# Triangular inverses of the RWKV-7 part: 32-blocks by substitution, or 16-blocks by substitution joined on TensorE

## The chip, the cores and the metric

The kernel runs on one core of a Trainium2 chip. The metric is the device time of one execution in microseconds (us). The kernel before takes 1602.5 us (median of three runs, 1602.16 to 1603.44). Its profile is one execution taken by the hardware profiler.

## What is computed

One layer of a hybrid decoder: a projection of 1024 tokens feeds an RWKV-7 head group (8 heads of 64) and an S5 state-space group. Their outputs are projected and added to the residual, and a SwiGLU FFN follows. The change touches only the recurrence of the RWKV-7 heads:

```
def step(S, inp):
    r_t, w_t, k_t, v_t, a_t, b_t = inp
    sa = einsum("bhvk,bhk->bhv", S, a_t)
    S = S * w_t[:, :, None, :] + sa[..., None] * b_t[:, :, None, :] + v_t[..., None] * k_t[:, :, None, :]
    y = einsum("bhvk,bhk->bhv", S, r_t)
    return S, y
_, y = lax.scan(step, S0, xs)
```

The kernel takes this recurrence in chunks of 64 tokens. Within a chunk the terms `sa` depend on each other through a strictly lower triangular 64x64 matrix, and the kernel needs the inverse of the unit triangular matrix belonging to it: for each of 8 heads and 16 chunks, so 128 inverses of 64x64.

## The kernel before

The tokens are taken in four quarters of 256 (`qt` 0 to 3), each with 4 chunks. A quarter has 16 units of two heads each (`u`; `h2` is the head within it), so 32 matrices of 64x64. For a quarter, `prepare` forms queries, keys and values, `post` does the rest before the chain of chunks, and `chains` then walks the four chunks one after another with small matmuls (`chunk`). Within `post` the steps are:

- `amats` (L942) forms the triangular matrices on TensorE in the tile `ak`, and `l_write` (L973) writes them to `l_d` in DRAM.
- `token_major` (L959) transposes keys and values on TensorE.
- `solve` (L980) loads from `l_d` the diagonal 32-blocks into `LU`, one block to a row. A block has 32 columns of its inverse, and two rows take 16 columns each, so 64 blocks fill 128 rows. A forward substitution of 31 steps follows, with a product (L995) and a sum (L997) in each: 62 instructions, each waiting for the one before. Quarters 0 and 1 run it on VectorE (DVE), quarters 2 and 3 on GpSimd (POOL) (L991). The inverse `X` and its transposed copy `VT` (L998) go to `x_d` in DRAM (L999, L1000).
- `rest` (L1002) loads them back with another layout (four DMAs, L1009 and L1010): a block's rows lie in 32 partitions, so that TensorE can use them. It joins two 32-blocks to a 64-block with two sets of 32 matmuls (`pG` L1017, `pO` L1027), ScalarE (ACT) evacuating both, and writes the result over the matrix in `ak` (L1032, L1035).

All loads and stores named here are issued by one queue, that of SyncE (SP), in order. Each engine works its instructions in order too. That order is fixed when the program is built, by a planner that simulates the engines' times; the text of the program gives the priority. Around the four solves the program weaves other work: quarter 0 with the second half of the input projection (`pz` matmuls of `zhalf`, L268) and S5 units; quarter 1 with the chain of quarter 0, the S5 gate (`pglu`) and the conditioning sums (`acc`, L293 and L295, of weights `wada`); quarters 2 and 3 with the first half of the FFN (`pgate`, `pup`, `pdn`, all at L268; L1352 evacuates `pdn` on DVE, L1382 takes `pup`).

PSUM has eight banks. `rest` draws its bank by `ps_g` (L111): the one bank `g`, or `g` and `G` in turn in one part of the run.

## Time and profile before

| What | Value |
|---|---|
| time, median of three runs | 1602.5 us |
| span of the profiled execution | 1598.3 us |
| PE, DVE, ACT, POOL busy | 1416.4, 988.7, 551.9, 540.9 us |

The profiled execution's span is 4.2 us under the median of the runs, which also hold what lies around the span. How to read the rows below: a timeline row gives the start, the busy time and the instruction, `x64` meaning 64 of them merged; in brackets stands the idle time just before on that engine and what ended it. `PEld` is TensorE's weight load, `PE` its matmul. A float32 matmul stands as two records, so the 32 matmuls of `pG` are 64. In rows by stretch, the first number is the stretch's length, then each engine's busy time with its instructions in brackets, then the granted TensorE clock (1.00 is full), the busy share of the DMA engines and GB/s.

### The profile page before, as it was taken

What the parts mean: (1) busy time and instruction counts of PE and PEld (TensorE: products, weight loads), DVE (VectorE), ACT (ScalarE), POOL (GpSimd) and SP (SyncE); (2) the same over time, 40 slices, a digit from 0 to 9 for tenths busy, and PEclk for the clock granted to TensorE, in tenths of its full rate; (3) what the DMA queues carried; (4) which work ended last, traced back from release to release, by engine and by line L of the source; (5) the groups of instructions that cost most, each with busy time, mean ns of one, the idle gap of its engine ahead of it and who ended that gap; (6) DMA issues with size and microseconds to landing.
All of it is one profiled execution on the core that took longest, in us unless ns stands there. A gap on an engine that the chain in (4) does not pass through costs nothing.

```text
span 1598.3 us, 23239 instructions
## 1 busy us (share of the span) xinstructions
PE 1416.4 (89%) x9167; PEld 1146.8 (72%) x9167; DVE 988.7 (62%) x1687; ACT 551.9 (35%) x881; POOL 540.9 (34%) x452
## 2 busy tenths in 40 slices
PE   3897798897958878698999999899997999999997
PEld 3675576776747756576777777677786888888885
DVE  5959458889686889854448855345626433433335
ACT  4341234344245653233225422224443222222223
POOL 4358344443053333145000003400251254444543
PEclk9897999999878989799999999899999999999999
DMA  9424674353454356353223224422831433232331
GB/s 277 146 79 143 171 233 152 109 134 100 93 161 129 122 177 196 115 116 97 66 67 113 86 88 106 97 68 68 222 104 50 137 93 105 81 105 92 99 99 53
DMA packets 266220, 189.78 MB, mean 119 GB/s; under 512 B 71670, under 2 KB 237184, under 8 KB 266112
## 3 DMA queue, kind: packets, MB, share of 16 engines
q1 hardware_dynamic: 264624, 186.65, 39.7%
q8 instruction: 72, 1.18, 0.3%
q0 software_dynamic: 816, 0.57, 0.2%
q10 hardware_dynamic: 672, 1.08, 0.2%
q14 instruction: 36, 0.29, 0.1%
HBM read 159.20 MB, written 31.16 MB: 119 GB/s over the span
## 4 chain that ended last, share of the span: by engine, by line
PE 56%; DVE 22%; DMA 8%; issue 5%; POOL 5%; ACT 2%; SPq 2%; DVEq 0%; POOLq 0%; ACTq 0%
PE pup L268 14%; PE pgate L268 13%; PE pdn L268 13%; PE pz L268 3%; DMA wada<-in_w_ada_dram 3%; PE p L1051 3%; DVE acc L295 2%; POOL XU L997 2%; POOL stmp L995 2%; PE pu L365 2%; PE po L1303 2%; DVE zo L864 1%; DVE stmp L995 1%; PE pA L951 1%; DVE XU L997 1%
## 5 line engine op out<-in xcount | busy, mean ns | idle before, releaser
L268 PE MATMUL pdn<-wd,act 128*128 128x512 f32 x1056 | 269.1, 397 | 0.7 <-DVE x L1352 0.6
L268 PE MATMUL pup<-h,hl_up 128*128 128x512 f32 x1056 | 268.6, 397 | 0.2 <-ACT hl_up L131 0.2
L268 PE MATMUL pgate<-h,hl_g 128*128 128x512 f32 x1056 | 264.1, 396 | 1.2 <-ACT hl_g L131 1.2
L1352 DVE TENSOR_TENSOR x<-pdn,x 128x512 f32<-128x512 f32 x176 | 119.0, 688 | 185.8 <-PE pdn L268 185.2
L268 PEld LDWEIGHTS pup<-h,hl_up 128*128 128x128 f32 x1056 | 198.1, 189 | 45.9 <-issue 2.6
L268 PEld LDWEIGHTS pdn<-wd,act 128*128 128x128 f32 x1056 | 196.6, 189 | 47.4 <-DVE x L1352 2.1
L268 PEld LDWEIGHTS pgate<-h,hl_g 128*128 128x128 f32 x1056 | 196.6, 188 | 47.4 <-issue 3.6
L268 PE MATMUL pz<-hT,hl_z 128*128 128x256 f32 (+1 forms) x1008 | 184.7, 340 | 37.0 <-ACT zt L859 20.8
L268 PEld LDWEIGHTS pz<-hT,hl_z 128*128 128x128 f32 x1008 | 154.7, 202 | 63.6 <-ACT zt L859 25.5
L1387 DVE TENSOR_TENSOR rawd<-rawd,gfb 128x1024 f32<-128x1024 f32 x44 | 54.9, 1248 | 101.2 <-DMA rawd<-in_ffn_w_down_dram 80.5
L1303 PE MATMUL po<-wo,yhl 128*128 128x512 f32 x384 | 99.1, 412 | 3.7 <-ACT wo L131 1.5
L131 ACT CAST hl_up<-raw_up 128x1024 fp32r<-128x1024 f32 x44 | 46.2, 1051 | 129.3 <-PE pup L268 110.2
L1303 PEld LDWEIGHTS po<-wo,yhl 128*128 128x128 f32 x384 | 74.6, 198 | 22.4 <-ACT wo L131 2.2
L131 ACT CAST wd<-rawd 128x1024 fp32r<-128x1024 f32 x44 | 45.7, 1049 | 117.6 <-DVE rawd L1387 86.8
L863 POOL TENSOR_TENSOR zo<-zt 128x512 f32<-128x512 f32 x28 | 40.9, 1461 | 109.9 <-ACT zt L859 107.2
L295 DVE SCALAR_TENSOR_TENSOR acc<-wada,cact,acc 128x256 f32<-128x256 f32 (+1 forms) x112 | 71.3, 644 | 5.4 <-DMA wada<-in_w_ada_dram 4.1
L127 POOL TENSOR_TENSOR yhl<-yt,yhl 128x512 fp32r<-128x512 f32 x16 | 23.9, 1494 | 149.4 <-ACT yhl L1288 144.1
L127 POOL TENSOR_TENSOR hl_g<-raw_g,hl_g 128x1024 fp32r<-128x1024 f32 x19 | 45.7, 2407 | 81.3 <-ACT hl_g L131 73.0
L1381 ACT ACTIVATE sgt<-pgate 128x512 f32<-128x512 f32 x44 | 26.4, 599 | 133.9 <-PE pgate L268 133.8
L995 POOL TENSOR_TENSOR stmp<-LU,XU 128x126 f32<-128x126 f32 (+22 forms) x62 | 28.0, 451 | 129.3 <-DMA LU<-l_d 124.6
L127 POOL TENSOR_TENSOR wd<-rawd,wd 128x1024 fp32r<-128x1024 f32 x19 | 50.4, 2654 | 54.6 <-ACT wd L131 54.6
L127 POOL TENSOR_TENSOR hl_up<-raw_up,hl_up 128x1024 fp32r<-128x1024 f32 x19 | 50.8, 2676 | 51.7 <-ACT hl_up L131 51.7
(372 smaller groups left out, 2453.6 us busy)
## 6 DMA issues: line engine op xcount, KB each, us to landing
raw_g<-in_ffn_w_gate_dram SPq DMA_DIRECT2D x44, 512.0 KB, 3.7
raw_up<-in_ffn_w_up_dram SPq DMA_DIRECT2D x44, 512.0 KB, 3.8
rawd<-in_ffn_w_down_dram SPq DMA_DIRECT2D x44, 512.0 KB, 3.5
wada<-in_w_ada_dram SPq DMA_DIRECT2D x64, 256.0 KB, 3.2
raw_z<-in_w_in_dram SPq DMA_DIRECT2D x28, 512.0 KB, 4.2
wada<-in_w_ada_dram SPq DMA_DIRECT2D x16, 512.0 KB, 7.9
wraw<-in_w_out_dram SPq DMA_DIRECT2D x32, 256.0 KB, 4.1
zt_d<-zo SPq DMA_DIRECT2D x28, 256.0 KB, 2.3
```

The source lines that it names most:

```text
L127: (eng or G).tensor_tensor(out=out, in0=a, in1=b, op=ALU.subtract)
L131: S.copy(dst[:, 0], src)
L268: PE.matmul(ps, lhsT=lf(a, k), rhs=rf(b, k), start=(n == 0), stop=(n == 3 * kb - 1))
L295: V.scalar_tensor_tensor(out=acc, in0=wt, scalar=cact[:, k:k + 1], in1=acc, op0=ALU.mult, op1=ALU.add)
L365: PE.matmul(pu[hf, b], lhsT=uw[b][:, a_, k, :], rhs=hT[hf, k][:, b_, :], start=(k == 0 and n == 0), stop=(k == 7 and n == 2))
L863: G.tensor_tensor(out=o, in0=zt[:, 0:HT], in1=zt[:, 1:HT + 1], op=ALU.subtract)
L995: SOLVE.tensor_tensor(out=t, in0=LU[:, j, j + 1:32].unsqueeze(2).to_broadcast([P, nt, nk]), in1=X[:, j:j + 1, 0:nk].to_broadcast([P, nt, n ...
L997: SOLVE.tensor_tensor(out=X[:, j + 1:32, 0:nk], in0=X[:, j + 1:32, 0:nk], in1=t, op=ALU.add)
L1051: PE.matmul(ps[r, h], lhsT=a, rhs=b, start=(n == 0), stop=(n == len(ops) - 1))
L1303: PE.matmul(pss[i], lhsT=yh[k][:, a, 128 * i:128 * i + 128], rhs=wo[:, b], start=(k == 4 and n == 0), stop=(k == 3 and n == 2))
L1352: V.tensor_tensor(out=t, in0=ps, in1=t, op=ALU.add)
L1387: V.tensor_tensor(out=raw, in0=raw, in1=gfb, op=ALU.mult)
```

## The change

`solve` takes 16-blocks: 128 rows hold the 128 diagonal 16-blocks of a quarter, all 16 columns of a block in its row. The substitution has 15 steps (30 instructions) on 16x16 tiles and runs on DVE in all four quarters. `LU` comes by one DMA with pieces of 64 bytes; `X` and its transpose are written to `x_d` by four DMAs with pieces of 64 bytes, into the diagonal halves of 32-blocks. `x_d` is now one buffer for all quarters, filled with zeros at the start by two DMAs of the POOL queue. `rest` loads two tiles with two DMAs, then joins 16-blocks to 32-blocks: `blocks` issues 64 matmuls of 32x32, four positions along the diagonal of the PE array, into one PSUM bank. It is called three times (`pH`, `pX`, `pV`), and DVE takes each result out, the first with a mask `mlow` made at the start by four POOL selects. After that `pG` and `pO` follow as before. Comments are removed as well.

```
+    mlow = const.tile([P, 32], F32, name="mlow")
+    V.memset(mlow, 0.0)
+    for b in range(4):
+        G.affine_select(out=mlow[32 * b:32 * b + 32, 0:16], in_=mlow[32 * b:32 * b + 32, 0:16], ..., fill=1.0)
...
-    x_d = dram.tile([4, 2, 65536], F32, name="x_d")
+    x_d = dram.tile([2, P, HT], F32, name="x_d")
...
+    zero = pp.tile([P, HT], F32, name="zero")
+    G.memset(zero, 0.0)
+    for n in range(2):
+        nc.gpsimd.dma_start(x_d[n], zero)
     s5_params(*s5q)
...
     def solve(qt):
-        LU, tmp = t_("LU", [P, 32, 32]), t_("stmp", [P, 256])
-        for o in range(2):
-            nc.sync.dma_start(LU[64 * o:64 * o + 64], l_d[qt][:, 0:2048].rearrange("r (i t) -> r i t", t=64)[:, :, 0:32])
+        LU, tmp, X, VT = t_("LU", [P, 16, 16]), t_("stmp", [P, 64]), t_("X16", [P, 16, 16]), t_("V16", [P, 16, 16])
+        nc.sync.dma_start(LU, l_d[qt].rearrange("r (x n) -> (r x) n", x=2)[:, 0:1024]
+                          .rearrange("r (i t) -> r i t", t=64)[:, :, 0:16])
...
-        SOLVE = V if qt < 2 else G
-        for j in range(31):
-            nt, nk = 31 - j, j // 2 + 1
+        for j in range(15):
+            nt, nk = 15 - j, j + 1
             t = tmp[:, 0:nt * nk].rearrange("p (a b) -> p a b", b=nk)
-            SOLVE.tensor_tensor(out=t, in0=LU[:, j, j + 1:32]..., in1=X[:, j:j + 1, 0:nk]..., op=ALU.mult)
-            SOLVE.tensor_tensor(out=X[:, j + 1:32, 0:nk], in0=X[:, j + 1:32, 0:nk], in1=t, op=ALU.add)
-        SOLVE.tensor_copy(VT.rearrange("p k i -> p i k"), X)
-        nc.sync.dma_start(x_d[qt, 0].rearrange("(r n) -> r n", r=P), X.rearrange("p i k -> p (i k)"))
-        nc.sync.dma_start(x_d[qt, 1].rearrange("(r n) -> r n", r=P), VT.rearrange("p k i -> p (k i)"))
+            V.tensor_tensor(out=t, in0=LU[:, j, j + 1:16]..., in1=X[:, j:j + 1, 0:nk]..., op=ALU.mult)
+            V.tensor_tensor(out=X[:, j + 1:16, 0:nk], in0=X[:, j + 1:16, 0:nk], in1=t, op=ALU.add)
+        V.tensor_copy(VT.rearrange("p k i -> p i k"), X)
+        for n, w in enumerate((X, VT)):
+            d = x_d[n].rearrange("(r s) (i k) -> s r i k", s=2, k=32)
+            for s_ in range(2):
+                nc.sync.dma_start(d[s_, :, :, 16 * s_:16 * s_ + 16], w[s_::2])
...
     def rest(qt):
-        for o in range(2):
-            src = x_d[qt, :, 32768 * o:32768 * o + 32768]
-            nc.sync.dma_start(XB[:, :, 16 * o:16 * o + 16], src[0].rearrange("(u p k) -> p u k", u=16, k=16))
-            nc.sync.dma_start(VB[o::2], src[1].rearrange("(u p i) -> p u i", u=16, i=32))
+        for n, w in enumerate((XB, VB)):
+            nc.sync.dma_start(w, x_d[n].rearrange("(u b) (i k) -> (b i) u k", u=16, k=32))
...
+        def blocks(nm, lf, rf):
+            ps = ps_g(nm).rearrange("p (u k) -> p u k", k=32)
+            for u in range(16):
+                for b in range(4):
+                    r = slice(32 * b, 32 * b + 32)
+                    PE.matmul(ps[r, u, :], lhsT=lf(r, u, b), rhs=rf(r, u), start=True, stop=True,
+                              tile_position=(32 * b, 32 * b))
+            return ps
+        ps = blocks("pH", lambda r, u, b: aks[u // 8][r, u % 8, 0, 0, 32 * (b % 2):32 * (b % 2) + 32], lambda r, u: XB[r, u, :])
+        V.tensor_tensor(out=GT, in0=ps, in1=mlow.unsqueeze(1).to_broadcast([P, 16, 32]), op=ALU.mult)
+        ps = blocks("pX", lambda r, u, b: VB[r, u, :], lambda r, u: GT[r, u, :])
+        V.tensor_tensor(out=XB, in0=ps, in1=XB, op=ALU.add)
+        ps = blocks("pV", lambda r, u, b: GT[r, u, :], lambda r, u: VB[r, u, :])
+        V.tensor_tensor(out=VB, in0=ps, in1=VB, op=ALU.add)
```

## Rows read from the trace of the kernel before

**Rows 1.** The page's busy times of the whole span, with their shares and instruction counts.

```profile
PE 1416.4 (89%) x9167; PEld 1146.8 (72%) x9167; DVE 988.7 (62%) x1687; ACT 551.9 (35%) x881; POOL 540.9 (34%) x452
```

**Rows 2.** Busy time by stretch, all engines: the stretches with solves 0 and 1 and what follows, then those with solves 2 and 3.

```profile
340.00:400.00 60.00, 49.57 (x371) 41.99 (x371) 59.17 (x112) 26.66 (x47) 31.55 (x16) 0.91 0.40 110
400.00:432.00 32.00, 29.58 (x242) 25.84 (x242) 21.93 (x61) 4.53 (x11) 2.20 (x3) 0.90 0.32 70
432.00:500.00 68.00, 45.72 (x671) 39.19 (x671) 51.38 (x130) 30.04 (x70) 28.14 (x42) 0.72 0.57 147
500.00:660.00 160.00, 127.55 (x1112) 99.68 (x1112) 139.82 (x278) 75.54 (x141) 57.75 (x50) 0.88 0.53 165
740.00:760.00 20.00, 14.96 (x179) 11.30 (x179) 8.48 (x13) 5.59 (x7) 3.06 (x10) 0.83 0.68 159
760.00:1018.00 258.00, 258.00 (x1627) 203.45 (x1620) 157.03 (x235) 85.06 (x120) 30.67 (x60) 1.00 0.30 87
1018.00:1040.00 22.00, 14.28 (x182) 11.75 (x181) 6.62 (x12) 4.26 (x8) 1.92 (x5) 0.77 0.48 96
```

**Rows 3.** The chain that ended last: its shares by line in the stretch 335 to 395 us and in 395 to 500 us.

```profile
by line: DVE stmp L995 16.6%; DVE f L736 9.8%; DVE L L729 9.4%; issue 8.6%; DVE XU L997 7.4%; DVE tm L968 5.8%; DVE zo L864 4.3%; PE pz L268 3.6%; DVE tm L725 3.3%; DVE kn L252 2.4%; DVE L L728 2.2%; DVE th L895 2.0%; DVE L L726 2.0%; DVE k
...
by line: PE pz L268 13.1%; DVE XU L997 12.0%; DVE stmp L995 9.0%; PE pY L752 7.0%; DMA wada<-in_w_ada_dram 6.7%; PE pA L951 5.4%; SPq L769 4.1%; PE pY L749 3.5%; PE pglu L268 3.3%; DMA VT<-x_d 3.2%; DMA l_d<-ak 2.9%; DVE acc L293 2.8%; DVE 
```

**Rows 4.** Busy time by stretch of the products alone (L995) for the four solves, then of the sums alone (L997) for solves 0 and 1: DVE, POOL, then the clock, DMA share and GB/s.

```profile
340.00:441.00 101.00, 14.71 (x31) 0.00 (x0) 0.88 0.43 103
441.00:482.50 41.50, 11.55 (x31) 0.00 (x0) 0.70 0.49 153
708.00:742.00 34.00, 0.00 (x0) 14.39 (x31) 1.00 0.30 83
982.00:1019.20 37.20, 0.00 (x0) 13.59 (x31) 1.00 0.24 74
...
340.00:441.00 101.00, 9.36 (x31) 0.00 (x0) 0.88 0.43 103
441.00:482.50 41.50, 14.79 (x31) 0.00 (x0) 0.70 0.49 153
```

**Rows 5.** Timeline of single instructions of solve 0: the last six, back to back; then one beside a POOL instruction, and one of like size alone.

```profile
424.19 0.21 DVE L995 TENSOR_TENSOR stmp<-LU,XU 128x45 f32<-128x45 f32 x1
...
425.33 0.18 DVE L997 TENSOR_TENSOR XU<-XU,stmp 128x16 f32<-128x16 f32 x1
...
389.49 2.82 POOL L127 TENSOR_TENSOR hl_z<-raw_z,hl_z 128x1024 fp32r<-128x1024 f32 x1
390.00 2.46 DVE L995 TENSOR_TENSOR stmp<-LU,XU 128x136 f32<-128x136 f32 x1
...
397.78 0.29 DVE L997 TENSOR_TENSOR XU<-XU,stmp 128x136 f32<-128x136 f32 x1
```

**Rows 6.** Busy time by stretch of `pG` alone (L1017) in quarters 1 and 2: PE, PEld, then the granted clock, DMA share and GB/s. Then the timeline of `pG`'s matmuls in all four quarters, with the wait before each.

```profile
489.00:491.00 2.00, 1.20 (x64) 1.09 (x64) 1.00 0.52 66
749.00:752.00 3.00, 1.92 (x64) 1.81 (x64) 0.50 0.95 199
...
432.55 1.20 PE L1017 MATMUL pG<-XU,ak 32*32 32x32 f32 x64 [1.66 <-DMA XU<-x_d]
489.59 1.20 PE L1017 MATMUL pG<-XU,ak 32*32 32x32 f32 x64 [1.42 <-DMA XU<-x_d]
749.59 1.92 PE L1017 MATMUL pG<-XU,ak 32*32 32x32 f32 x64 [5.04 <-DMA XU<-x_d]
1025.98 1.92 PE L1017 MATMUL pG<-XU,ak 32*32 32x32 f32 x64 [7.72 <-DMA XU<-x_d]
```

**Rows 7.** Timeline of FFN weight loads just after those two long waits, and one group some us later; then one group that changes the tile shape between FFN matmuls.

```profile
751.43 5.76 PEld L268 LDWEIGHTS pup<-h,hl_up 128*128 128x128 f32 x19
1028.87 3.02 PEld L268 LDWEIGHTS pdn<-wd,act 128*128 128x128 f32 x9
1031.93 1.57 PEld L268 LDWEIGHTS pup<-h,hl_up 128*128 128x128 f32 x7
...
757.55 0.73 PEld L890 LDWEIGHTS pw<-wzk,wa 64*128 64x128 f32 x4 [0.35 <-issue]
```

**Rows 8.** A PSUM evacuation with a mask on DVE (minimum, median and maximum in ns of all 32), and the transposed copy of solve 0.

```profile
L953 DVE TENSOR_TENSOR ak<-pA,mask x32: 673/686/692, 281.6 to 971.4; 128x512 f32<-128x512 f32 x32
...
425.55 0.61 DVE L998 COPY VT<-XU 128x512 f32<-128x512 f32 x1
```

**Rows 9.** DMA issues (count, KB each, median us from issue to landing), then the SP queue's own time for one issue (ns, minimum, median, maximum) of `x_d`'s writes and of the loads into `LU`.

```profile
LU<-l_d SPq DMA_DIRECT2D x8, 256.0 KB, 4.7
XU<-x_d SPq DMA_DIRECT2D x8, 128.0 KB, 4.5
...
L999 SPq DMA_DIRECT2D x_d<-XU x4: 325/338/339, 425.5 to 1019.1; - x4
...
L987 SPq DMA_DIRECT2D LU<-l_d x8: 592/872/1767, 339.0 to 976.1; - x8
```

**Rows 10.** Timeline of POOL in the start-up: four mask selects, four DMA issues, and the idle time before a later instruction.

```profile
3.59 0.92 POOL L151 TENSOR_SCALAR_AFFINE_SELECT mask<-mask 64x64 f32<-64x64 f32 x4
...
122.24 2.15 POOL L638 DMA_DIRECT2D dcol<-in_s_d_dram  x4
...
96.35 2.40 POOL L127 TENSOR_TENSOR hl_z<-raw_z,hl_z 128x1024 fp32r<-128x1024 f32 x1 [7.26 <-ACT hl_z L131]
```

More of the change, by code (lines that the diff above doesn't have):

```diff
@@ L159 @@
         V.memset(rm[32 * b:32 * b + 32, b % 2:b % 2 + 1], 1.0)
+    mlow = const.tile([P, 32], F32, name="mlow")
+    V.memset(mlow, 0.0)
+    for b in range(4):
+        G.affine_select(
+            out=mlow[32 * b:32 * b + 32, 0:16], in_=mlow[32 * b:32 * b + 32, 0:16], pattern=[[0, 16]], base=16,
+            channel_multiplier=-1, compare_op=ALU.is_gt, fill=1.0,
+        )
     m01 = const.tile([P, HT], F32, name="m01")
@@ L982, in solve @@
         t_ = lambda nm, sh: RP[0].tile(sh, F32, tag=nm, name=nm)
-        LU, tmp = t_("LU", [P, 32, 32]), t_("stmp", [P, 256])
-        X, VT = (RP[0].tile([P, HT], F32, tag=nm, name=nm) for nm in ("XU", "VT"))
-        X, VT = X.rearrange("p (i k) -> p i k", k=16), VT.rearrange("p (k i) -> p k i", i=32)
-        for o in range(2):
-            nc.sync.dma_start(LU[64 * o:64 * o + 64], l_d[qt][:, 0:2048].rearrange("r (i t) -> r i t", t=64)[:, :, 0:32])
-        G.memset(X, 0.0)
-        for o in range(2):
-            G.memset(X[64 * o:64 * o + 64].rearrange("p i k -> p (i k)")[:, 16 * o:512:33], 1.0)
@@ L999, in solve @@
-        nc.sync.dma_start(x_d[qt, 0].rearrange("(r n) -> r n", r=P), X.rearrange("p i k -> p (i k)"))
-        nc.sync.dma_start(x_d[qt, 1].rearrange("(r n) -> r n", r=P), VT.rearrange("p k i -> p (k i)"))
-    def rest(qt):
-        XB, VB, GT = (t.rearrange("p (u k) -> p u k", k=32) for t in
-                      [RP[0].tile([P, HT], F32, tag=nm, name=nm) for nm in ("XU", "VT")] + [tr("GT")])
-        for o in range(2):
-            src = x_d[qt, :, 32768 * o:32768 * o + 32768]
-            nc.sync.dma_start(XB[:, :, 16 * o:16 * o + 16], src[0].rearrange("(u p k) -> p u k", u=16, k=16))
-            nc.sync.dma_start(VB[o::2], src[1].rearrange("(u p i) -> p u i", u=16, i=32))
-        aks = [sts[qt, q]["ak"] for q in range(2)]
+        LU, tmp, X, VT = t_("LU", [P, 16, 16]), t_("stmp", [P, 64]), t_("X16", [P, 16, 16]), t_("V16", [P, 16, 16])
@@ new lines, in solve @@
+        nc.sync.dma_start(LU, l_d[qt].rearrange("r (x n) -> (r x) n", x=2)[:, 0:1024]
+                          .rearrange("r (i t) -> r i t", t=64)[:, :, 0:16])
+        G.memset(X, 0.0)
+        G.memset(X.rearrange("p i k -> p (i k)")[:, 0:256:17], 1.0)
+        for j in range(15):
+            nt, nk = 15 - j, j + 1
+            t = tmp[:, 0:nt * nk].rearrange("p (a b) -> p a b", b=nk)
+            V.tensor_tensor(out=t, in0=LU[:, j, j + 1:16].unsqueeze(2).to_broadcast([P, nt, nk]),
+                            in1=X[:, j:j + 1, 0:nk].to_broadcast([P, nt, nk]), op=ALU.mult)
+            V.tensor_tensor(out=X[:, j + 1:16, 0:nk], in0=X[:, j + 1:16, 0:nk], in1=t, op=ALU.add)
@@ new lines, in solve @@
+        V.tensor_copy(VT.rearrange("p k i -> p i k"), X)
[3 more added lines that the diff above has]
+                nc.sync.dma_start(d[s_, :, :, 16 * s_:16 * s_ + 16], w[s_::2])
+    def rest(qt):
+        XB, VB = (t_.rearrange("p (u k) -> p u k", k=32) for t_ in
+                  [RP[0].tile([P, HT], F32, tag=nm, name=nm) for nm in ("XU", "VT")])
+        GT = tr("GT").rearrange("p (u k) -> p u k", k=32)
+        for n, w in enumerate((XB, VB)):
+            nc.sync.dma_start(w, x_d[n].rearrange("(u b) (i k) -> (b i) u k", u=16, k=32))
+        aks = [sts[qt, q]["ak"] for q in range(2)]
+        def blocks(nm, lf, rf):
[12 more added lines that the diff above has]
+        V.tensor_tensor(out=VB, in0=ps, in1=VB, op=ALU.add)
@@ L1020, in rest @@
             p0 = 64 * h2 + 32
-            S.copy(GT[p0:p0 + 32].rearrange("p u (k o) -> p u o k", o=2),
-                   ps[p0:p0 + 32].rearrange("p u (o k) -> p u o k", o=2))
+            S.copy(GT[p0:p0 + 32], ps[p0:p0 + 32])
         ps = ps_g("pO").rearrange("p (u k) -> p u k", k=32)
```

2 lines of the change are left out of this document (removed).

## The prediction

> **What bounds the kernel now.** I read the page's busy times first. PE is busy 1416.4 of 1598.3 us, DVE 988.7, POOL 540.9 [rows 1]. Those are means over stages with different limits, so next I cut the run into stretches around the solves [rows 2]. From 340 to 400 us DVE works 59.17 of 60 us and PE idles 10.4: DVE ends last. From 400 to 432 PE works 29.58 of 32: PE ends last. From 432 to 660 neither is full; DVE works 51.38 of 68 and 139.82 of 160, and latencies and loads lie between. From 740 to 1040 PE is busy throughout but for two holes: 5.04 us in 740 to 760 and 7.72 us in 1018 to 1040. The chain that ended last says the same with names [rows 3]: in 335 to 395 it is mostly DVE, and the solve's two lines hold 16.6% and 7.4% of it; in 395 to 500 it starts on `pz` and `pA` of PE, and later the solve of quarter 1 holds 12.0% and 9.0%. Solves 2 and 3 matter in another way: POOL works at them through 34 and 37 us [rows 4] while PE has FFN matmuls to do, and only the tail shows, as `pG` waiting for the loaded inverses [rows 6].
>
> So the change has two halves. In quarters 0 and 1 it takes work from an engine that is the bound. In quarters 2 and 3 it takes work from an idle engine (POOL) and gives some to PE, which is the bound.
>
> **Early: quarters 0 and 1.** Solve 0 costs DVE 14.71 + 9.36 = 24.07 us in 62 instructions, solve 1 11.55 + 14.79 = 26.34 [rows 4], and the transposed copy 0.61 us in solve 0 [rows 8]. Afterwards there are 30 instructions of at most 64 elements. The cheapest price is the step of the last small ones, six from 424.19 to 425.51: some 0.22 us each, so 6.6 us [rows 5]. The dearest is the present mean, 26.34 / 62 = 0.42 us: 12.7 us. The mean lies so far above the bottom because an instruction that meets a POOL instruction can take far longer: 2.46 us beside a POOL instruction of 2.82 us, where one of equal size takes 0.29 [rows 5]. POOL's other work stays, so I take a middle price of 0.33 us: 10 us per solve. Half the present copy comes to 0.3 us, and three PSUM evacuations of 0.69 us like that of `pA` to 2.1 [rows 8]. DVE pays 12.4 us instead of about 24.7 and 27: 12 and 15 us less.
>
> Not all of it is on the path. Of solve 0 the chain holds 24% of 60 us, 14.4 us, up to 395 [rows 3]. The 30 new instructions would mostly fall in that same stretch, at 10 us, so 4.4 us are won there. The rest of solve 0 lies beside PE's `pz` work and wins nothing. On the other side the joins of quarter 0 may land in that PE-bound stretch of 400 to 432; today `pG` runs after it. They cost at most 6.7 us (worked out below), and I take 2 us as exposed. Quarter 0 gives -2 us, with -10 (PE's whole idle time to 400) and +7 as ends.
>
> Of solve 1 the chain holds 21% of 105 us, 22 us. In its place come 10 us of solve, 0.3 of copy and 2.1 of evacuations: -9.6. Two delays stand against it. The DMAs: `X` and its copy now leave by four issues with 64-byte pieces instead of two; nothing in the trace writes such pieces, so I bound an issue by a write of long rows (0.34 us) below and a median issue into `LU` (0.87 us) above [rows 9]: 0.7 to 2.8 us more of SP's queue, behind which weight loads such as `wada` wait, which hold 6.7% of the chain from 395 to 500 [rows 3]. The two loads of 256 KB that replace four of 128 KB take the landing time of `LU` (4.7 us) against 4.5, and half the issues. I take +1.5. The joins: a set of matmuls, a hand-over, 0.69 us of DVE and a hand-over, three times, about 10 us more before `ak` is ready. But the solve now takes 41.5 us from first to last instruction [rows 4], and with 38% of its DVE time it should end 15 to 20 us sooner; that covers the 10. Quarter 1 gives -8 us, with -15 (all of DVE's saving) and 0 as ends. Early sum: -10.
>
> **Late: quarters 2 and 3.** PE's added work is three sets of 64 matmuls per quarter, 128 records each. Today's 64 records take 1.09 us of weight loads at full clock, 17 ns each, 1.81 at half [rows 6]. They alternate between two positions of the array; the new sets use four, which no row shows. If four overlap twice as well, a set takes 1.1 us; if not, 2.2; at half clock 3.6. I take 2.2, the nearest row: 6.7 us per quarter, 13.4 for both (6.6 to 21.6). Each set also cuts into a row of FFN matmuls, twice; a cut costs up to 0.35 us of unexplained issue time [rows 7]. Six sets and twelve cuts are 4.2 us at most; some sets will follow each other, so I take 2.
>
> The Trainium skill, "TensorEngine Tiling (Array Packing)", section Key Properties, says that a change of the tiling mode, not just of the tile, drains TensorE. That speaks against small sets amid 128x128 matmuls; the gap of 0.35 us before the 64-row group agrees in kind [rows 7]. If every change cost it, late would come out about 2 us dearer.
>
> Won back are the two waits of `pG` for the inverses, 5.04 and 7.72 us, and what follows them at half clock: 19 loads in 5.76 us and 9 in 3.02, against 0.224 us each in the group at 1031.93 [rows 7], 1.5 and 1.0 us, and 0.7 us for each `pG`: 3.9. Together 16.7 us. Why did PE wait? The planner put `pG` where it thought the data would be there, and POOL was late. The two quarters whose solves run on DVE waited only 1.66 and 1.42 us [rows 6]. With solves 2 and 3 on DVE, and POOL nearly empty from 760 to 1018 (30.67 us, solve 3 nearly alone [rows 2]), I expect waits of some 2.5 us each, new small ones at `pX`, `pV` and `pG` included, since each now waits for a DVE instruction in order behind FFN instructions. Won: 12 us. So late: +13.4 + 2 - 12 = +3.4.
>
> DVE itself takes on some 10 us per quarter there: it works 157.03 of 258 us from 760 to 1018 [rows 2], so the work is covered by idle time; uncovered it would cost 20. The new waits on DVE are the ones for `LU` and for the three sets: behind each stand `pdn`'s evacuations, and then PE, whose FFN has one bank each for `pgate` and `pup` and two for `pdn`. I add 0.6 us. Late sum: +4 (-10 to +16).
>
> The Trainium skill, "SBUF — State Buffer", section SBUF: two separate sides, says that VectorE instructions with two SBUF inputs and GpSimd instructions lock each other out of one port pair for a whole instruction. The 2.46 us agree [rows 5]. By that rule alone late solves on DVE cost the bottom price, 6.6 us.
>
> **Start-up.** Four more selects on POOL, 0.92 us for four like them, and two DMA issues on POOL's queue, 0.5 us each by the four issues of 2.15; POOL idles 7.26 us before 96.35 [rows 10]. Cover: DMA waits and that idle time. I put 0; uncovered, 0.9 + 1.1 + a memset, 2.5 us.
>
> **The sum.** -10 + 4 = -6 us: 1592.3 of span. The runs lie 4.2 us above the profiled span, left as it is: 1596.5 us.
>
> **Rivals.** (A) Early gain carried in full. If the stretch 432 to 660 is really bound by DVE, all 12 + 15 us go at quarters 0 and 1, less the 10 of latency that the joins add, and the waits of quarters 2 and 3 vanish: -17 early, 13.4 + 2 + 0.6 - 16.7 = -1 late, about 1585. For it: DVE at 87% from 500 to 660 [rows 2]. Against: the chain crosses `wada` loads.
> (B) A new bound takes the place of DVE. If `wada`'s loads and PE's `pz` set the early end, early wins 5 at most and late takes it: 1601.5, no change. For it: PE has only 2.4 us of idle time in 400 to 432.
> (C) Slower: the joins on PE. `pH` waits for loads as long as `pG` did (12.8 us), because the planner sets the new 64-byte DMAs too short; the four later steps wait too. Then nothing is won late, and 13.4 of joins, 4 of cuts and 4 of waits at the later steps (four steps, two quarters, 0.5 each) are added: +21. With early at -10 that is +11, 1613; with early at -14, +7, 1609. It decides from a wait of 6 us per quarter at `pH`.
>
> **Chances.** Forecast 0.45 (1589 to 1600), A 0.13, B 0.16, C 0.26. Measurement of this kernel tells about 0.2%, 3.2 us, from no change. Faster: A and most of the forecast, 0.54; same: B and its edge, 0.18; slower: C and the edge of B, 0.28. The range takes in A and the lower half of C: 1583 to 1610; the forecast's own is 1589 to 1600.
>
> **What would show it.** Right: DVE's time at the two lines falls to about 10 us per solve early and 7 late; the set of 128 records takes 2.2 us at full clock; the wait before `pH` in the FFN stage is under 3 us; 340 to 660 shrinks by some 10 us and the FFN stretch from 700 on, at equal work, grows by some 4. Wrong: `pH` waits over 6 us, DVE is not fuller where it is freed but PE idles as before, or DVE's wait for `LU` shows up as idle time on PE.

## The result and the profile after

The changed kernel takes 1625.3 us (median of four runs, 1619.9 to 1630.9) against 1602.3 for the kernel before: ratio 1.013, 95% interval 1.009 to 1.017. It is slower by 23 us where 6 us less were forecast. Its profiled execution took 1623.63 us, with a span of 1621.9. A second set of runs gave 1628.9 us, ratio 1.015 (1.012 to 1.018).

The page's busy times of the changed kernel (those of before: [rows 1]):

```profile
PE 1446.1 (89%) x10703; PEld 1159.1 (71%) x10703; DVE 983.0 (61%) x1698; ACT 542.8 (33%) x875; POOL 477.5 (29%) x329
```

PE has 1536 matmul records more and is busy 29.7 us longer. DVE is 5.7 us lower, although it now does all four solves; POOL is 63.4 us lower. PE's idle time doesn't grow with the span: it falls from 181.9 to 175.8 us, so the longer span is PE being busy longer, not PE waiting longer. Twelve join sets at the 1.29 us shown below account for some 15.5 us of the 29.7; the rest, some 14 us, is the work that PE had before, taking longer. The stretches of [rows 2], in the changed kernel (columns as there):

```profile
340.00:400.00 60.00, 49.53 (x498) 41.85 (x498) 59.01 (x118) 27.25 (x51) 25.00 (x17) 0.97 0.46 116
400.00:432.00 32.00, 31.68 (x650) 27.01 (x652) 22.61 (x41) 7.35 (x15) 3.46 (x3) 0.95 0.16 44
432.00:500.00 68.00, 52.47 (x1032) 46.29 (x1030) 34.00 (x88) 27.22 (x67) 28.82 (x39) 0.77 0.49 125
500.00:660.00 160.00, 124.90 (x993) 94.30 (x988) 129.75 (x256) 72.18 (x132) 58.01 (x50) 0.85 0.50 153
740.00:760.00 20.00, 18.15 (x344) 13.73 (x343) 11.82 (x19) 5.28 (x11) 0.44 (x2) 0.91 0.55 107
760.00:1018.00 258.00, 255.98 (x1955) 200.48 (x1954) 163.58 (x270) 82.07 (x118) 0.11 (x1) 1.00 0.31 86
1018.00:1040.00 22.00, 20.88 (x409) 17.03 (x408) 11.53 (x18) 7.66 (x12) 0.00 (x0) 1.00 0.33 98
```

From 432 to 500 us DVE is emptier (34.00 against 51.38), as forecast, yet what follows does not come sooner. The two holes of the FFN stretch are nearly gone: PE works 18.15 of 20 and 20.88 of 22.

The new work cost what the next rows show. Busy time of the products (L1003), then of the sums (L1005), in the stretches with solves 0 to 3 (columns as in [rows 4]; here the busy time is DVE's):

```profile
340.00:400.00 60.00, 5.09 (x15) 0.97 0.46 116
400.00:448.00 48.00, 3.07 (x15) 0.89 0.20 45
690.00:745.00 55.00, 3.07 (x15) 0.97 0.42 100
975.00:1012.00 37.00, 3.09 (x15) 1.00 0.45 101
...
340.00:400.00 60.00, 5.57 (x15) 0.97 0.46 116
400.00:448.00 48.00, 3.08 (x15) 0.89 0.20 45
690.00:745.00 55.00, 3.10 (x15) 0.97 0.42 100
975.00:1012.00 37.00, 3.05 (x15) 1.00 0.45 101
```

Solve 0 takes 5.09 + 5.57 = 10.7 us, the other three 6.1 to 6.2 each. Timeline of join sets on PE, of quarters 0, 2, 2 and 3 (start, busy, instruction, wait before it):

```profile
394.98 1.29 PE L1028 MATMUL pH<-XU,ak 32*32 32x32 f32 x128 [0.78 <-DMA XU<-x_d]
...
745.49 0.99 PE L1028 MATMUL pH<-XU,ak 32*32 32x32 f32 x92
...
757.25 1.29 PE L1028 MATMUL pX<-GT,VT 32*32 32x32 f32 x128
...
1020.94 1.29 PE L1028 MATMUL pX<-GT,VT 32*32 32x32 f32 x128
```

A set of 128 records takes 1.29 us at full clock, and in the FFN no set of these rows waits for data; `pG` had waited 5.04 and 7.72 us [rows 6]. So the solves and joins are cheaper than forecast, and yet 23 us are lost.

Where? I put six landmarks through every run: **f**, the first scan of the S5 units on DVE (no solve has begun); **y**, the last store of the S5 gate to `y_d`; **fin**, the last product of quarter 1 (`ld`, DVE); **po**, the first out-projection matmul; **gate**, the first FFN matmul (`pgate`); and **end**, the last evacuation of `pdn`. Each is the start of a row of the trace, in us. The median beside them is that of the timed runs, the ratio that to the kernel before (whose median lay between 1602.2 and 1603.6 in all comparisons), with its 95% interval; the landmarks come from one profiled execution each.

| Kernel | median | ratio | f | y | fin | po | gate | end |
|---|---|---|---|---|---|---|---|---|
| before | 1602.3 | | 248.9 | 568.7 | 597.2 | 582.8 | 685.7 | 1590.2 |
| changed | 1625.3 | 1.013 (1.009, 1.017) | 255.6 | 578.9 | 599.5 | 598.9 | 703.5 | 1613.5 |
| after_again | 1628.9 | 1.015 (1.012, 1.018) | 252.4 | 585.4 | 607.6 | 607.0 | 712.2 | 1621.2 |
| e1_startup | 1630.7 | 1.017 (1.015, 1.019) | 256.9 | 577.8 | 619.9 | 591.2 | 712.0 | 1620.6 |
| e2_pad | 1618.7 | 1.008 (1.005, 1.011) | 250.2 | 581.0 | 606.6 | 593.6 | 703.7 | 1612.3 |
| e3_late | 1627.0 | 1.015 (1.012, 1.018) | 249.8 | 583.0 | 625.2 | 597.2 | 717.2 | 1622.9 |
| e4_early | 1609.3 | 1.004 (1.003, 1.006) | 249.6 | 567.4 | 575.8 | 581.7 | 683.0 | 1597.8 |
| p1_mask | 1614.6 | 1.007 (1.005, 1.009) | 250.5 | 574.5 | 604.6 | 586.7 | 696.9 | 1606.1 |
| p2_zero | 1608.8 | 1.003 (1.002, 1.005) | 251.2 | 573.2 | 604.8 | 587.4 | 693.2 | 1595.1 |
| e5_clean | 1597.7 | 0.997 (0.996, 0.998) | 248.2 | 568.1 | 584.2 | 583.2 | 684.6 | 1584.5 |
| e6_proj | 1629.0 | 1.016 (1.014, 1.018) | 251.0 | 572.4 | 618.0 | 586.3 | 709.7 | 1614.6 |
| e7_late | 1596.4 | 0.997 (0.996, 0.999) | 247.7 | 569.2 | 597.6 | 583.1 | 686.0 | 1586.1 |
| e8_early | 1614.0 | 1.007 (1.005, 1.009) | 249.5 | 573.3 | 595.4 | 586.1 | 700.9 | 1604.7 |
| e9_zero | 1602.4 | 1.001 (0.999, 1.002) | 250.9 | 570.3 | 589.1 | 588.5 | 689.0 | 1584.6 |
| m1_mask_later | 1609.7 | 1.004 (1.002, 1.006) | 252.2 | 583.1 | 602.0 | 601.4 | 704.2 | 1607.7 |
| p5_mask_later | 1609.1 | 1.004 (1.002, 1.005) | 246.6 | 569.3 | 598.9 | 586.0 | 689.3 | 1599.0 |
| f1_sums | 1624.5 | 1.013 (1.012, 1.015) | 251.9 | 584.4 | 594.2 | 597.0 | 717.8 | 1617.8 |
| g1_clean_sums | 1610.7 | 1.004 (1.003, 1.006) | 248.2 | 569.0 | 579.6 | 581.9 | 698.4 | 1601.9 |
| p3_swap | 1602.6 | 1.001 (0.999, 1.002) | 246.9 | 569.2 | 596.4 | 581.9 | 685.2 | 1591.5 |
| p4_clean_swap | 1598.7 | 0.998 (0.996, 0.9996) | 249.7 | 572.0 | 587.9 | 587.1 | 688.9 | 1590.6 |

In the changed kernel's trace the 23.3 us at the end are made of 6.7 before any solve begins (f), 3.5 more up to y, 5.9 between y and po, 1.7 between po and gate, and 5.5 in the FFN. In after_again they are 3.5, 13.2, 7.5, 2.3 and 4.5, together 31.0. No single place holds the loss, and the places differ between two executions of one program.

Two of the pieces can be read in rows. First the start-up. Timeline of the changed kernel, one POOL instruction and the DVE instruction that stands beside it, then two DVE instructions later:

```profile
148.13 4.35 POOL L612 TENSOR_TENSOR s5tw<-pwr,bb 128x2048 f32<-128x2048 f32 x1
...
148.65 4.92 DVE L127 TENSOR_TENSOR hl_z<-raw_z,hl_z 128x1024 fp32r<-128x1024 f32 x1
...
171.30 2.05 DVE L127 TENSOR_TENSOR hl_z<-raw_z,hl_z 128x1024 fp32r<-128x1024 f32 x1
173.28 2.88 DVE L876 SCALAR_TENSOR_TENSOR zo<-zo,cols,zt 128x512 f32<-128x512 f32 x1
```

The same DVE instructions in after_again:

```profile
148.21 4.92 DVE L127 TENSOR_TENSOR hl_z<-raw_z,hl_z 128x1024 fp32r<-128x1024 f32 x1
...
170.87 1.21 DVE L127 TENSOR_TENSOR hl_z<-raw_z,hl_z 128x1024 fp32r<-128x1024 f32 x1
172.00 0.74 DVE L876 SCALAR_TENSOR_TENSOR zo<-zo,cols,zt 128x512 f32<-128x512 f32 x1
```

and the first of them in the kernel before:

```profile
148.53 1.63 DVE L127 TENSOR_TENSOR hl_z<-raw_z,hl_z 128x1024 fp32r<-128x1024 f32 x1 [0.17 <-ACT hl_z L131]
```

The split of a weight block (`hl_z`) takes 4.92 us beside POOL's product of 4.35 us, and 1.63 before. The later pair takes 2.05 + 2.88 us in the one execution and 1.21 + 0.74 in the other: 3.0 us of the difference of 3.2 in f. Which DVE instructions meet a POOL instruction thus differs between the two kernels, and between two executions of one program.

Second, the hand-over to the out-projection. Timeline of PE in the kernel before:

```profile
581.24 2.08 PE L1110 MATMUL pg<-gs,g2w 128*128 128x256 f32 x4 [0.79 <-DVE lsq L1096]
582.75 6.47 PE L1303 MATMUL po<-wo,yhl 128*128 128x512 f32 x24
...
592.48 1.02 PE L1110 MATMUL pg<-gs,g2w 128*128 128x256 f32 x4
```

and in the changed kernel:

```profile
586.41 2.08 PE L1135 MATMUL pg<-gs,g2w 128*128 128x256 f32 x4 [0.78 <-DVE lsq L1121]
597.41 2.08 PE L1135 MATMUL pg<-gs,g2w 128*128 128x256 f32 x4 [8.93 <-DVE ld L1136]
598.92 5.29 PE L1328 MATMUL po<-wo,yhl 128*128 128x512 f32 x16
```

Before, 24 `po` records start between the two groups of `pg`. In the changed kernel's order both groups of `pg` stand ahead of `po`: PE waits 8.93 us for DVE's last product of quarter 1, and the out-projection, whose data could be there, waits behind it. The planner set that order.

### The profile page after: what moved, and what is told of

Its sections match the earlier page's. It is cut to its first block, busy times and chain, and to the rows that moved or that the text cites. A ratio compares the mean times of both kernels' runs of the same rounds, so it can differ in the third digit from the quotient of the medians.

```text
span 1621.9 us, 26171 instructions
## 1 busy us (share of the span) xinstructions
PE 1446.1 (89%) x10703; PEld 1159.1 (71%) x10703; DVE 983.0 (61%) x1698; ACT 542.8 (33%) x875; POOL 477.5 (29%) x329
## 4 chain that ended last, share of the span: by engine, by line
PE 58%; DVE 20%; DMA 10%; issue 5%; ACT 3%; POOL 2%; SPq 2%; POOLq 0%; DVEq 0%; ACTq 0%
PE pgate L276 14%; PE pdn L276 13%; PE pup L276 13%; PE p L1076 3%; PE pz L276 3%; DVE acc L303 2%; DMA wada<-in_w_ada_dram 2%; PE po L1328 2%; PE pu L373 2%; PE pA L963 2%; DMA rawd<-in_ffn_w_down_dram 1%; PE ptr L1354 1%; DVE f L748 1%; DMA yt<-y_d 1%; PE pglu L276 1%
## 5 line engine op out<-in xcount | busy, mean ns | idle before, releaser
L276 PE MATMUL pdn<-wd,act 128*128 128x512 f32 x1056 | 272.5, 398 | 5.4 <-ACT act L131 2.2
L276 PE MATMUL pgate<-h,hl_g 128*128 128x512 f32 x1056 | 269.5, 400 | 2.2 <-ACT hl_g L131 1.9
L276 PE MATMUL pz<-hT,hl_z 128*128 128x256 f32 (+1 forms) x1008 | 191.3, 347 | 39.9 <-ACT zt L871 17.7
L276 PEld LDWEIGHTS pz<-hT,hl_z 128*128 128x128 f32 x1008 | 158.6, 207 | 67.8 <-ACT zt L871 21.6
L127 POOL TENSOR_TENSOR wo<-wraw,wo 128x512 fp32r<-128x512 f32 x32 | 43.4, 1360 | 63.6 <-ACT wo L131 56.0
```

The costliest lines, as they stand in the source:

```text
L127: (eng or G).tensor_tensor(out=out, in0=a, in1=b, op=ALU.subtract)
L276: PE.matmul(ps, lhsT=lf(a, k), rhs=rf(b, k), start=(n == 0), stop=(n == 3 * kb - 1))
```

## The experiments

**First, which part loses.** The start-up additions alone, put into the kernel before:

```diff
+    mlow = const.tile([P, 32], F32, name="mlow")
...
+    for n in range(2):
+        nc.gpsimd.dma_start(zf_d[n], zero)
```

> The kernel before with the change's start-up additions alone: the mask mlow, and the zero tile with its two DMAs on POOL's queue, which here fill a buffer that nothing reads. In the trace after the change everything from 226 to 380 us stands 7.0 us later than before. Theory S (these additions make that delay): the first load of B_d starts about 195 instead of 189 us, and the time is 1607 to 1610. Rival (the delay comes of the order in which the planner set things because of the later parts of the change, or is luck): B_d within 1 us of before and the time 1601 to 1604.

1630.7 us. Every solve is as before, and the kernel is as slow as with the whole change. Theory S was right that these additions cost, and far too low: 8.0 us at f, near the 7.0 expected, and 18 more between po and gate, 120.8 against 102.9 us.

Next, the changed kernel without the zero fill:

```diff
-        nc.gpsimd.dma_start(x_d[n], zero)
...
-                nc.sync.dma_start(d[s_, :, :, 16 * s_:16 * s_ + 16], w[s_::2])
+                nc.sync.dma_start(d[s_], w[s_::2, :, 16 - 16 * s_:48 - 16 * s_])
```

> The changed kernel without the zero fill: the 16-blocks are solved inside tiles of 48 columns whose outer 32 are zero, and the four DMAs to x_d write 32 columns each, 16 of the block and 16 of zeros, in pieces of 128 bytes. mlow stays. Theory S (the zero fill costs the 7 us of the start-up): 1617 to 1620, with B_d's first load back at 189 us. Rival (64-byte pieces to x_d or their contention hold up the solves' results): the write of x_d lands sooner than 3.3 us and the joins start earlier by over 2 us. Rival (neither matters): 1622 to 1628.

1618.7 us, as theory S had it, and f is back at 250.2. But its nine runs lie between 1605 and 1624 us and the profiled one took 1622.8, so the median alone hardly separates theory S from the last rival.

And the two halves of the change, each with the start-up additions:

```diff
-        solve(qt)
+        (solve if qt >= 2 else solve_b)(qt)
```

> The change in quarters 2 and 3 alone, its start-up additions included; quarters 0 and 1 solve 32-blocks as before. Theory O (the loss of some 12 to 16 us sits in the early part, where joins and the chain of quarter 0 overtake the second half of the projection, whose end the S5 gate and the conditioning sums wait for): 1602 + 7 of start-up + 3 to 7 of late joins = 1612 to 1616, and the gate's first tanh comes within 3 us of 466 (before's 458.8 plus the start-up). Rival L (the joins amid the FFN cost what the prediction's slower rival says): 1619 to 1626.

> The change in quarters 0 and 1 alone, its start-up additions included; quarters 2 and 3 solve 32-blocks on POOL as before. Theory O: 1602 + 7 of start-up + 10 to 14 = 1618 to 1623, with the last zo of the second half of the projection near 457 us and the gate's first tanh near 480. Rival L (the loss is late): 1605 to 1611.

1627.0 us for the late half and 1609.3 for the early half: theory O has them the wrong way round. Rival L's numbers (1619 to 1626, 1605 to 1611) come near, but not its cause: in e3_late the loss does not lie where the change is. On PE its order is that of e1_startup up to solve 2, and gate comes at 717.2 us, 31.5 late; gate to end takes 905.7, 1.2 us more than before.

**Then the start-up additions taken apart, and taken out.** p1_mask has the mask alone, p2_zero the zero fill alone, in the kernel before. e5_clean is the whole change with the mask made just before solve 0 and the padded write of e2_pad. e6_proj alters the weave of the changed kernel:

```diff
-    weave((post(0), 1), (prepare(1), 2), LIM(zg, 1))
+    weave((post(0), 1), (prepare(1), 2), (zg, 1))
```

> The kernel before with the mask mlow alone (one memset on DVE, four selects on POOL at the start; nothing reads it). The start-up additions together took the kernel before to 1630 us, though every solve stayed as it was. Theory P (the additions move the planner's simulated times by a fraction of a microsecond, it puts the rest of the program into another order, and this order is worse; the work itself is cheap): a time away from 1602 by 5 us or more, 1607 to 1632, and like e1_startup a longer stretch from the first out-projection matmul to the first FFN tanh than the 111 us of before. Rival Z (the work of the zero fill costs it): 1601 to 1604.

> The kernel before with the zero tile and its two DMAs on POOL's queue alone, into a buffer that nothing reads; no mask. Rival Z (the work of the zero fill itself costs it): 1625 to 1632, as with both. Theory P (order, not work): any value from 1600 to 1632; the delay before 226 us in its trace is not tied to the zero DMAs, and the parts that lose time lie after 450 us, where no zero fill runs.

> The whole change with its start-up additions taken out: the mask is made just before solve 0, and the zeros come with the padded write of e2_pad. Up to some 230 us its order is that of the kernel before. If the loss of 23 us were the start-up's (7 us of delay and what follows from it), the time is 1596 to 1603, the prediction's own. Theory O (the joins and the chain of quarter 0 overtake the second half of the projection, and the S5 gate starts late): 1612 to 1619, last pz at 450 us or later against 427.8 before.

> The changed kernel with one word of its weave altered: all blocks of the second half of the projection are woven with the post step of quarter 0, so that on PE the last pz stands at place 1751 of 7893 (place 1735 of 7125 before, 2113 in the changed kernel). Theory O: last pz returns from 457 to 430-436 us (with the start-up's 7 us), the gate's first tanh to 462-468, and the time to 1606 to 1613. Rival (the early loss is from the joins' own latency and DMAs, or from bad luck in the order behind them): no better than 1620.

The mask alone costs 11 us (1614.6), the zero fill 5 (1608.8): rival Z falls. In p1_mask the landmarks are 1.6 us late at f and 11.2 late at gate. The built programs say why to look there: of PE's 7125 instructions several hundred (522 when told apart by the tile that they write) stand at another place than before, 20 of those in the start-up and the others between instruction 1,935 and 2,810, which run from about 475 to 670 us. e5_clean takes 1597.7 us and is faster than the kernel before. Theory O falls with it: its last `pz` starts at 448.0 us (427.8 before), and the kernel is fast all the same. e6_proj says so from the other side: it brings the last `pz` back to 423.8 us, and quarter 1 then is finished at 618.0; 1629.0 us.

**The halves again, without start-up additions;** and the change with the zero fill kept and the mask made at solve 0.

```diff
+        if qt == 2:
+            make_mlow()
+        (solve if qt >= 2 else solve_b)(qt)
```

> The change in quarters 2 and 3 alone, without start-up additions (mask made before solve 2, zeros by the padded write; quarters 0 and 1 as before). On PE the order is that of the kernel before up to solve 2. The prediction's late term: +4, 1606. Theory S (only the start-up additions lose time, and the late part wins what the clean kernel's trace shows from the first FFN matmul to the end, 5 us): 1596 to 1600, first FFN matmul within 2 us of 685.7. Rival: the DVE-solved quarters 2 and 3 make the FFN's DVE instructions late, 1603 to 1610.

> The change in quarters 0 and 1 alone, without start-up additions (mask made before solve 0, padded write); quarters 2 and 3 on POOL as before. The prediction's early term: -10, 1593. Theory S with the clean kernel's trace (first FFN matmul 684.6 against 685.7 before, though quarter 1 finishes 12 us sooner, because the S5 gate starts later and the conditioning sums take their 62 to 67 us after it): -1 to -3, 1600 to 1602. Rival: early as e4_early, 1607 to 1611.

> The changed kernel with the mask alone moved to solve 0; zero fill at the start-up and 64-byte writes as in the change. If mask and zero fill add up one by one (clean kernel 1598, zero fill +5 in the kernel before, mask +21 on top of the padded kernel): 1600 to 1606. If the two start-up additions lose time only together, or the 64-byte writes cost what the padded ones don't: 1612 or more.

The late half alone wins: 1596.4 us, and gate to end falls from 904.5 to 900.1. Busy time by stretch in e7_late, the stretches of [rows 2] with solves 2 and 3:

```profile
740.00:760.00 20.00, 20.00 (x404) 15.97 (x402) 11.67 (x17) 7.15 (x10) 0.86 (x2) 1.00 0.39 118
760.00:1018.00 258.00, 256.44 (x2037) 201.17 (x2037) 164.35 (x268) 81.63 (x118) 0.85 (x2) 1.00 0.32 87
1018.00:1040.00 22.00, 22.00 (x251) 17.63 (x251) 11.06 (x18) 5.71 (x10) 0.00 (x0) 1.00 0.23 69
```

Timeline of the end of one of its sets, and of two whole sets:

```profile
733.80 0.31 PE L1022 MATMUL pH<-XU,ak 32*32 32x32 f32 x4 [2.39 <-issue]
...
741.51 1.29 PE L1022 MATMUL pX<-GT,VT 32*32 32x32 f32 x128
...
754.32 1.20 PE L1037 MATMUL pG<-XU,ak 32*32 32x32 f32 x64
```

PE is full where it had holes, 20.00 of 20 and 22.00 of 22 us. One hole of 2.39 us stands before these stretches, inside quarter 2's first set; the profile shows nothing that PE waited for there. The early half alone loses 12 us (1614.0), outside of all that was expected of it, while both halves together (e5_clean) win 5. In e8_early po comes at 586.1 and gate 114.8 us after it; in e5_clean at 583.2 and 101.4. The halves don't add up. e9_zero, 1602.4, is no different from the kernel before.

**Place or work of the mask, and the queue of the sums.** m1_mask_later and p5_mask_later make the mask with the same instructions behind the parameter loads, in the changed kernel and in the kernel before:

```diff
-    mlow = const.tile([P, 32], F32, name="mlow")
     m01 = const.tile([P, HT], F32, name="m01")
...
     nc.gpsimd.dma_start(g2w, rw_g2[0])
+    mlow = const.tile([P, 32], F32, name="mlow")
```

f1_sums (the changed kernel) and g1_clean_sums (e5_clean) set the last conditioning sums ahead:

```diff
-    weave((LIM(late, 16), 2), o0, (LIM(adl, 2), 1))
+    weave((adl, 2), (LIM(late, 16), 2), o0)
```

> The changed kernel with the lines that make the mask moved down in the program, behind the parameter loads; the same instructions, still in the start-up, zero fill kept. On PE the order then is that of e9_zero from the first to the last instruction. Theory P (the mask costs by its place: the planner's times shift and it orders the middle of the run otherwise): as e9_zero, 1599 to 1606. Rival W (the mask's work costs, wherever it is in the start-up): 1618 to 1628, as the change.

> The kernel before with the mask's instructions at that later place; nothing reads it. All engines keep the order of the kernel before, with one memset and four selects more. Theory P: 1601 to 1604 (the mask ahead of the loads took 1614.6). Rival W: 1611 to 1618.

> The changed kernel, start-up as it is, with the last conditioning sums (parts 4 and 5) woven ahead of the out-projection and of quarter 2's preparation instead of behind them. In the changed kernel's trace the loads of wada pause from 627 to 640 us, while DVE waits 5.4 us for pn, which stands on PE behind out-projection matmuls; the first FFN matmul comes 103.5 us after quarter 1 is finished, against 89 before. If the loss of the middle is this queue: the first FFN matmul comes 8 to 14 us sooner, 690 to 696, and the time is 1608 to 1616. If the out-projection then comes late instead by as much: 1620 to 1628.

> e5_clean with the same weave of the last sums. There the first FFN matmul came 100.6 us after quarter 1 was finished. If the queue is what eats quarter 1's gain of 13 us: first FFN matmul 674 to 678, time 1587 to 1592, faster than both kernels. If not: 1595 to 1600.

Moving the mask's lines gives back 15.6 of the changed kernel's 23 us (1609.7), with the same instructions in the start-up: theory P, mostly. But its order on PE is that of e9_zero from end to end, and e9_zero takes 7.3 us less. And p5_mask_later keeps the order of the kernel before on every engine, with five instructions more, and takes 1609.1: nearer to rival W than to P. So order is not all. Its f is 2.3 us early, its gate 3.6 late and its end 8.8 late. Busy time by stretch of the kernel before, then of p5_mask_later:

```profile
430.00:500.00 70.00, 46.38 (x675) 39.61 (x675) 53.19 (x134) 30.96 (x73) 28.14 (x42) 0.72 0.59 147
500.00:600.00 100.00, 85.04 (x934) 66.47 (x934) 83.53 (x170) 58.78 (x107) 39.76 (x36) 0.90 0.49 151
600.00:690.00 90.00, 67.91 (x380) 54.18 (x380) 76.38 (x144) 25.90 (x47) 29.09 (x22) 0.87 0.49 151
```

```profile
430.00:500.00 70.00, 51.19 (x671) 43.79 (x671) 50.51 (x126) 29.75 (x69) 27.79 (x42) 0.63 0.58 144
500.00:600.00 100.00, 86.59 (x928) 66.22 (x928) 81.39 (x169) 58.89 (x108) 39.84 (x36) 0.86 0.48 145
600.00:690.00 90.00, 67.05 (x372) 54.19 (x371) 76.91 (x148) 25.14 (x46) 28.64 (x22) 0.85 0.51 150
```

The counts of the instructions nearly agree, and the granted clock is lower in all three stretches: 0.63 against 0.72, 0.86 against 0.90, 0.85 against 0.87. That is the part up to gate. The other 5 us are lost later, where the clock is full. Busy time by stretch in the FFN, the kernel before, then p5_mask_later:

```profile
1250.00:1500.00 250.00, 250.00 (x1093) 204.86 (x1092) 94.94 (x110) 62.90 (x76) 115.56 (x45) 1.00 0.32 97
```

```profile
1250.00:1500.00 250.00, 250.00 (x1077) 201.21 (x1076) 92.72 (x107) 61.97 (x76) 109.80 (x43) 1.00 0.32 98
```

PE is always busy at the full clock in both, and gets 16 matmuls fewer done in p5_mask_later. Counted by work: from the 1,701st to the 3,151st FFN matmul, in the same order everywhere, PE takes 333.7 us in nine of the traces of the table and 338.6 or 338.7 us in the other eleven, with none between. The eleven are those whose kernels make `mlow` in the pool `const` in the start-up, ahead of the loads or behind them; the nine have no mask or make it just before a solve, in the pool of the solves. So 5.0 us come with the mask's tile. Neither the order nor the granted clock carries them: the kernel before and p5_mask_later have the same order on PE, and so have e9_zero and m1_mask_later, and each pair shows the 5.0 us. In the built programs the mask's tile in `const` takes 128 bytes of each partition to the end of the run, and all tiles of the FFN's pool `fp`, among others, lie 128 bytes further on in those eleven. That this shift is what slows the matmuls is not shown, since no run moved the tiles and did nothing else.

The pair e9_zero and m1_mask_later shows what the lower clock costs at one place. Busy time by stretch around 400 us, first e9_zero, then m1_mask_later:

```profile
392.00:396.00 4.00, 0.74 (x4) 0.74 (x5) 4.00 (x6) 0.89 (x2) 0.60 (x2) 0.95 0.41 66
396.00:400.00 4.00, 4.00 (x20) 3.38 (x18) 3.93 (x9) 1.28 (x1) 0.00 (x0) 0.63 0.18 66
400.00:424.00 24.00, 23.74 (x560) 20.02 (x560) 15.53 (x26) 5.49 (x11) 3.46 (x3) 1.00 0.19 47
```

```profile
392.00:396.00 4.00, 0.51 (x58) 0.40 (x44) 4.00 (x4) 0.64 (x2) 2.24 (x2) 1.00 0.52 78
396.00:400.00 4.00, 3.69 (x14) 3.25 (x15) 3.93 (x8) 1.54 (x2) 0.00 (x0) 0.52 0.19 68
400.00:424.00 24.00, 24.00 (x203) 18.49 (x202) 11.32 (x18) 2.51 (x4) 3.46 (x3) 0.51 0.12 34
```

and the first instructions after PE's wait and the set `pV`, up to which both have done the same work, e9_zero, then m1_mask_later:

```profile
395.26 1.62 PE L269 MATMUL pz<-hT,hl_z 128*128 128x256 f32 x7 [3.80 <-ACT zt L864]
...
414.37 1.29 PE L1033 MATMUL pV<-VT,GT 32*32 32x32 f32 x128
```

```profile
396.31 1.86 PE L269 MATMUL pz<-hT,hl_z 128*128 128x256 f32 x7 [3.80 <-ACT zt L871]
...
425.20 1.29 PE L1028 MATMUL pV<-VT,GT 32*32 32x32 f32 x128
```

Both orders are the same and both wait 3.80 us. Then PE is busy nearly without a break in both. In the one execution it runs the stretch from 400 to 424 us at 2.4 GHz, in the other at 1.2 GHz (0.51). The same work, from the end of the wait to the start of `pV`, takes 19.1 us in the one and 28.9 in the other. (The 560 and 203 records of the rows are not equal work: many of the 560 are of 32x32 sets that the slower execution had still to come to.) m1_mask_later's profiled run is one of its slower ones (1604 to 1621 us) and e9_zero's its fastest (1595 to 1611), so the pair shows what a run can lose there, not the difference of the medians. after_again has the same row as m1_mask_later: 0.51 from 400 to 424 us.

The queue of the sums isn't the place of the loss: f1_sums stays at 1624.5 us, and g1_clean_sums is 13 us slower than e5_clean. The sums came sooner, and what they were set ahead of came later: gate 718 and 698 us.

**Last, how far a build moves when nothing is added,** and the changed kernel once more. p3_swap and p4_clean_swap set five small memsets of `rm` ahead of those that make `mask2`, in the kernel before and in e5_clean:

```diff
+    rm = const.tile([P, 2], F32, name="rm")
     mask2 = const.tile([P, 2, 64], F32, name="mask2")
...
-    rm = const.tile([P, 2], F32, name="rm")
```

> The kernel before with the lines that make rm (five small DVE memsets) set ahead of those that make mask2: no work added, and all engines but DVE's first twenty instructions in the same order. If only added work moves the time: 1601 to 1604. If a shift of early instructions by tenths of a microsecond is enough to move it, as p5_mask_later's 5.6 us suggest: away from 1602 by 3 us or more, either way.

> e5_clean with the same swap. If its gain is the change's: 1594 to 1601. If it was a lucky build: 1602 or more.

> The changed kernel as it is, once more. Time 1620 to 1630. If the delay before 226 us is part of this program, the first f of the S5 units starts near 255.6 us again; if it is a matter of one execution, near 251, as in f1_sums, whose start-up is the same.

p3_swap stays where the kernel before is (1602.6), p4_clean_swap where e5_clean is (1598.7, ratio 0.998). So not every shift moves the time, and the clean kernel's gain of 4 to 6 us outlasts one. But both swaps leave PE's order as it was, so they don't test the gain in another order. In after_again f comes at 252.4: half of the delay of 6.7 us belongs to the program, the rest to one execution.

## Why the prediction was wrong

**Start-up: the step that failed.** It was put at 0, with 2.5 us as the dear end, since POOL idles and the instructions are short. The instructions are short, and the step still cost the result: 1630.7 us with these additions alone, 1597.7 with all of the change but them. It was costed as work and had to be costed as a disturbance. By the medians, which come from different sets of runs, the way from the clean kernel (1597.7 us) to the changed one (1625.3) has three parts: 4.7 us for the zero fill with the 64-byte writes (e9_zero), 7.3 more for the mask made in the start-up behind the loads (m1_mask_later), and 15.6 more for making it ahead of them.

The 15.6 us go with the mask's place: that is shown, since the instructions are the same. The kernel's order is made by a planner from simulated times; five small instructions ahead of the parameter loads, in the first 4 us of the run, shift those times, and a stretch more than 400 us later comes out in another order (p1_mask). The same work between po and gate takes from 100 to 123 us in these kernels. That the new order is the means is only argued, from the loss and the moved instructions lying in the same stretch; it was not shown by running one order with and without the mask. Of the 7.3 us, order has no part: PE's order is the same in both. 5.0 us of them lie in the last stretch of the FFN, at the full clock, and come with the mask's tile being kept in `const`; the same 5.0 stand in p5_mask_later's 5.6. What is left of either goes along, in the traces, with a lower granted clock before gate. How the 15.6 us divide between order, clock and DVE's meetings with POOL stays open, and so does why the kept tile slows matmuls in that one stretch.

**Early sum, -10.** Nearly nothing of it arrives at gate in e5_clean (-1.1 us). The solves were priced well: 10.7 us for solve 0 (10 taken), 6.2 for solve 1. Quarter 1 is finished 13 us sooner, near the 12 to 15 that DVE saves. But po stays (582.8 and 583.2), and so does y (568.7 and 568.1); in no run of the table does po follow y by less than 12 us. I read that as the bound (from the table): I followed the chain of quarter 1 and didn't ask what else the out-projection needs: the S5 gate, whose start waits for the second half of the projection, which the joins and the chain of quarter 0 now overtake. The traces bear this out in part: in every trace with the new early solves but e6_proj's, y follows the last `pz` by 118.6 to 122.5 us, while that `pz` moves from 447.4 to 464.0 us. But e6_proj, whose weave brings it back to 423.8 us, has y at 572.4, no sooner than the kernel before (568.7), so another bound that no run found lies close behind. That is the first half of rival B, a new bound: `pz`, which B named, by way of the S5 gate, which it didn't. In e8_early the early half even loses 12 us; why it does alone and not beside the late half stays open beyond the longer stretch from po to gate.

**Late sum, +4.** e7_late measures -5.8 us by the medians, -4.6 by the ratio. Two terms were mis-sized. The set of 128 records takes 1.29 us, not 2.2: four positions of the array overlap, near the lower bound of 1.1. Six sets are 7.7 us instead of 13.4 (six times 2.2 is 13.2, a slip without effect). And the two waits are gone, 16.7 us with their half clock, where I kept 5 back for new ones: in e7_late one hole of 2.39 us stands in their place. With the cuts at 2 and DVE's waits at 0.6 the sum would have been -6.4, and with this hole -4.0; from gate to end e7_late's trace wins 4.4. The Trainium skill's drain at a change of tiling mode ("TensorEngine Tiling (Array Packing)", Key Properties) shows no trace: in e7_late PE has no idle time around three sets in 740 to 760 us, and the hole of 2.39 us lies inside a set. In the changed kernel itself gate to end took 5.5 us more; e1_startup, whose late part is untouched, took 4.1 more, so this is not the joins: the 5.0 us of the kept mask tile stand in both.

**The rivals.** C was the slower one, decided by `pH` waiting 6 us for its loads; `pH` waits 0.78 us in quarter 0, 1.46 in quarter 1 and not at all in the FFN, and C is refuted though the sign was its own. A is refuted with the early sum. The sum of -6 agrees with e5_clean's -6.0 by luck: two errors cancel, early too good and late too bad.

**Other marks.** Issues of the 64-byte pieces took 0.59 to 0.68 us each, within 0.34 to 0.87. The solves late in the run took 6.1 to 6.2 us each, a little under the bottom price of 6.6. The stretch 340 to 660 didn't shrink.

## What to carry to other kernels

Where a planner orders the program, cost an early edit as a disturbance of all that follows, not only as work: put helper constants where they move nothing, and compare the order of the built programs before the time. Here the mask made just before its use, in the pool of the solves, cost nothing that shows in e5_clean and e7_late; behind the loads it still cost 5.6 to 7.3 us, 5.0 of them in a stretch more than 1200 us away. So look at what stays allocated too, and time a stretch of equal work at the full clock before you put a loss down to order or clock. Before you call saved time won, list everything that the next stage waits for; here quarter 1 came 13 us sooner and the gate beside it not at all. Of the versions tried the one with the new solves in quarters 2 and 3 alone is the fastest (1596.4 us, ratio 0.997), with the whole change without its start-up additions equal to it within the intervals.
